# Seven products for both halves of the columns, with their sums of weights made in DRAM ahead of time

## The chip, the cores and the metric

The kernel runs on one core of a Trainium2 chip. A core has TensorE (PE in the profile, with its weight loads shown apart as PEld), VectorE (DVE), ScalarE (ACT), GpSimd (POOL) and SyncE (SP), and 16 DMA engines that all queues share. The metric is the device time of one execution in microseconds. The kernel before takes 2182.1 us (median of three runs, 2181.91 to 2182.17).

## The reference, cut to what matters

Two layers on 256 tokens of width 2048, all in float32. Layer 0 mixes with attention and pooling, layer 1 with an mLSTM, and each mixer is followed by a gated MLP:

```
x = x + mixed                                    # attention layer, then mLSTM layer
x = x + conv_ffn(rms_norm(x, norm_ffn[layer]), w_up[layer], conv_w[layer], conv_b[layer], w_down[layer])

u = x @ w_up                                     # 2048 -> 2 * 5632
u = c[0] * up[:, :-2] + c[1] * up[:, 1:-1] + c[2] * up[:, 2:] + conv_b
gate, val = jnp.split(u, 2, axis=-1)
return (jax.nn.silu(gate) * val) @ w_down        # 5632 -> 2048
```

The change concerns the last product, `(256 x 5632) @ (5632 x 2048)`.

## The kernel before, in words

**Products.** Every float32 operand is split into a high part and a rest, and a product is three matmuls: high by high, high by rest, rest by high. The activations are split once. The weights stream from DRAM in tiles of 128 x 1024 (512 KB): `Stream` loads a tile on SP's queue up to five tiles ahead, and splits it up to two tiles ahead (`split`, L110 to L126: a cast on ACT, L121, and a subtraction on DVE, L122). There are six buffers for raw and four for split tiles.

**The MLP.** The 44 blocks of 128 hidden columns are worked in six chunks (`FCH`, of 4, 8, 8, 8, 8, 8 blocks). For each block an up-projection takes four weight tiles (64 matmuls, `up`), then gather, convolution and gating run on ACT and DVE. While chunk c is projected up, the down product of chunk c - 1 is woven between its up-projections, in the order that `_ffn_plan` writes out. The output columns are four blocks of 512. Columns of the first half (blocks 0 and 1) come from plain blocks (`down`, tile `dn`): 8 K blocks x 2 row blocks x 3 matmuls = 48 a block.

**Seven products.** The second half of the columns (`_halves` gives `(1,)`) uses a form of block multiplication in which a 2 x 2 by 2 x 2 product takes seven block products instead of eight. A pair of K blocks, the two row blocks of 128 and the two column blocks of 512 make up the 2 x 2 blocks. `combine` forms sums of activations for a pair. `unit` of kind "A" does four products that need sums of weights, kind "B" three with plain weights. With weight blocks b11, b12, b21, b22 the A products need b11 + b12, b12 + b22, b11 + b12 + b22 and the sum of all four. These are formed as the tile arrives: a `Sum` tile is loaded by SP and the second summand is added by an accumulating DMA on POOL's queue (`prepare`, L104 to L108); the next tile, a `Chain`, is completed with two additions on DVE (L117, L118). A products collect in four PSUM banks, go to the accumulator `acc` or to the residual `x`, and `total` puts the accumulator together at the end. The last chunk uses plain blocks for all columns.

**Order.** PE runs in program order. A small clock, `Weave`, interleaves side tasks (generators, such as a head of attention) with the main stream: each matmul group advances it by its own time, and a task that yields d is resumed when d us of it have passed. So a task's delay sets where its instructions stand in the program. On ACT, DVE, POOL and SP the framework's planner (`schedule_with_timeline_sim=True`, L1325) then orders the instructions by a timeline of its own and by their data; only the very beginning is kept in program order on ACT, DVE and SP as well. Each engine executes its list in order, DMA issues included. A DMA issue waits on semaphores first: for its data and buffers, and for an earlier DMA that used the same completion semaphore.

**POOL's other work.** POOL computes the power -1/2 of every norm (`rsqrt`, L245): `ry_n0` for the first norm, `ry_qk` for the keys, `ry_qq0`, `ry_qq1`, `ry_qq2` for three blocks of four query heads. DVE multiplies with the result right after (L247 to L250).

Of the kernel before, what the change touches and what calls it, by code (L numbers as in the profile page):

```python
# [16 lines left out]
P = 128  # L17
# [14 lines left out]
FT = DFF // P  # L32
FCH = [4, 8, 8, 8, 8, 8]
CH = 8
BOTH = ()
NEG = -1.0e30
NGATE = 96 + 8
WARM = 5
# [31 lines left out]
        self.one, self.other = one, other  # L70


class Chain:


# [4 lines left out]
class Stream:  # L80
# [8 lines left out]
    def load(self, pieces=1):  # L89
        i = self.n_load  # L90
        self.n_load += 1
        src = self.srcs[i]
        if isinstance(src, Sum):
            i in self.w or self.prepare(i)
            return
        src = src.src if isinstance(src, Chain) else src
        width = src.shape[-1]
        n = width // pieces
        w = self.wpool.tile([P, CH * P], F32, tag="w", name=f"w{i}")
        for c in range(0, width, n):  # L100
            self.nc.sync.dma_start(w[:, c : c + n], src[:, c : c + n])
        self.w[i] = w, n, width

    def prepare(self, i):  # L104
        w = self.sums.tile([P, CH * P], F32, tag="sum", name=f"sum{i}")
        self.nc.sync.dma_start(w, self.srcs[i].one)
        self.nc.gpsimd.dma_start(w, self.srcs[i].other, accum_op=ALU.add)
        self.w[i] = w, CH * P, CH * P  # L108
# [80 lines left out]


@with_exitstack
def trunk(ctx: ExitStack, tc: tile.TileContext, gx, xT, xn, call, catt, cml, weights, out):
    nc = tc.nc
    v, a, g, pe = nc.vector, nc.scalar, nc.gpsimd, nc.tensor

# [506 lines left out]
    def mlstm_layer(norm, nxt):  # L702
        with ExitStack() as es:
# [171 lines left out]

            hns, done = {}, set()
            wv.add(norm.finish(), 6.0)
            for hp in range(MH // 2):
                vf = t1p.tile([P, 2, 512], F32, tag="vf", name=f"mvf{hp}")
                for c, n in ((0, MD + 32), (MD, MD)) if hp == 0 else ((0, 512),):  # L880
                    ps = mov_group(xx, f"mv{hp}_{c}", n)
                    if hp + c == 0:
                        wv.until(lambda: norm.rcol is not None)
                        wv.add(gates(ps))
                    n = min(n, 512 if hp else MD)
                    for t in range(2):
# [12 lines left out]
                wv.add(gated(mov_group(xx, f"mo{hp}"), [2 * hp, 2 * hp + 1]))  # L899
# [7 lines left out]
    def ffn_layer(layer, norm, nxt):  # L907
        with ExitStack() as es:
# [16 lines left out]
            def up(c, f, gt, i):  # L925
# [156 lines left out]

            wv.add(norm.finish(), 4.0)
            f, gts = 0, []
            for kind, c, i, *j in _ffn_plan():
                if kind == "up":
                    if i == 0:
                        gts.append(actp.tile([P, 8, 2, S], F32R, tag=f"B{c % 2}", name=f"g{layer}_{c}"))
                    up(c, f, gts[c], i)
                    f += 1  # L1090
                elif kind == "down":
                    down(c, i)
                elif kind == "two":
                    down_two(c)
                elif kind == "mix":
                    combine(c, i)
                else:
                    unit(kind, c, i, *j)
# [58 lines left out]
    return np.ascontiguousarray(t.transpose(4, 0, 2, 1, 3, 5)).reshape(FT * (KT // 4), P, CH * P)  # L1157


def _halves(c):  # L1160

    return () if c == len(FCH) - 1 else (0, 1) if c in BOTH else (1,)


def _ffn_plan():

    seq = []
    for c, n in enumerate(FCH):
        pairs = FCH[c - 1] // 2 if c else 0
        units = [(kind, c - 1, h, j) for h in (_halves(c - 1) if c else ()) for kind in "AB" for j in range(pairs)]
        per = max(1, len(units) // n)

        busy = {u[3]: k // per for k, u in enumerate(units) if u[0] == "A"}
        for i in range(n):
            seq.append(("up", c, i))
            seq += units[i * per : i * per + per]  # L1180
            if len(_halves(c - 1)) == 1:
                for b in range(2):
                    if pairs and i == (b + 1) * pairs // 2 - 1:
                        seq.append(("down", c - 1, b))
# [5 lines left out]
def _down_chunks(w):  # L1190


    out, k0 = [], 0
    for c, n in enumerate(FCH):
        rows = w[k0 * P : (k0 + n) * P]
        blocks = [_mov(rows[:, b * 512 : b * 512 + 512]) for b in range(NB) if b // 2 not in _halves(c)]
# [15 lines left out]
    return res  # L1212


def _ffn_weights(up, parts):

    down = iter(parts[0])
    out, u = [], 0
    for kind, c, i, *j in _ffn_plan():
        if kind == "up":  # L1220
            out += up[u : u + 4]
            u += 4
        elif kind in ("down", "two"):
            out += [next(down) for _ in range(FCH[c] // 2 * (2 if kind == "two" else 1))]
        elif kind != "mix":
            s0, s1, r, ba, bb = parts[1 + 5 * i : 6 + 5 * i]
            q = sum(FCH[:c]) // 2 + j[0]
            out += [Sum(s0[q], s1[q]), Chain(r[q])] if kind == "A" else [ba[q], bb[q]]
    return out


def _constants():
# [97 lines left out]
```

## Time and profile before

| | |
|---|---|
| median of three runs | 2182.1 us |
| the profiled execution | 2182.76 us, span 2181.0 us |
| PE busy | 2175.4 us (100%) |
| DVE busy | 1670.8 us (77%) |
| ACT busy | 1370.6 us (63%) |
| POOL busy | 59.3 us (3%) |
| DMA | 462.95 MB, mean 212 GB/s |
| granted TensorE clock | 1.0 |

The span is the profiled execution on the core itself; 1.8 us lie around it. By the timeline of PE attention ends at some 256 us, the first MLP at 975 us, the mLSTM layer at 1457 us, and the second MLP fills the rest. In lines of groups and of the timeline, `out<-in` names the tiles that are written and read, L121 is line 121 of the kernel, and what stands in brackets is the engine's idle time just before and what ended it. Rows of engine SPq, ACTq or POOLq are DMA issues on these queues.

### The profile page before, as it was taken

To read this page: it belongs to the slowest core of one execution; us is meant where nothing else is said; L and a number is where in the kernel's file an instruction comes from. 1 tells how busy PE (TensorE), PEld (TensorE's weight loads), DVE (VectorE), ACT (ScalarE), POOL (GpSimd) and SP (SyncE) were. 2 spreads that over 40 slices of the span, in tenths; PEclk is the share of its full clock that TensorE was granted. 3 is DMA by queue.
4 is the path that set the end of the run, shared out by engine and by line. 5 is a ranking of instruction groups with operands and counts; after the bars stand their busy time and mean duration, and the time that the engine had idled before them with its cause. 6 is when DMAs were issued, how large, how long until landed. Compare 5 with 4: busy or idle time off the path is not lost.

```text
span 2181.0 us, 31219 instructions
## 1 busy us (share of the span) xinstructions
PE 2175.4 (100%) x11508; PEld 1862.8 (85%) x11508; DVE 1670.8 (77%) x2366; ACT 1370.6 (63%) x2166; POOL 59.3 (3%) x76
## 2 busy tenths in 40 slices
PE   9999999999999999999999999999999999999999
PEld 7888888888888888889888888888888888888887
DVE  7686688887878788776777676668888787878776
ACT  7665576766767576666454554557676666757663
POOL 0010000000000000000000000000000000000000
PEclk9999999999999999999999999999999999999999
DMA  9556567676877766656465555756768677776664
GB/s 326 178 169 203 174 199 235 206 244 206 256 226 245 229 221 215 219 193 205 160 201 182 180 179 175 223 182 197 232 205 243 214 240 236 242 230 227 215 213 163
DMA packets 133595, 462.95 MB, mean 212 GB/s; under 512 B 14810, under 2 KB 17154, under 8 KB 133442
## 3 DMA queue, kind: packets, MB, share of 16 engines
q1 hardware_dynamic: 125024, 438.08, 60.0%
q0 software_dynamic: 5344, 19.14, 5.2%
q10 hardware_dynamic: 3074, 3.75, 0.7%
q8 instruction: 90, 1.47, 0.3%
q14 instruction: 63, 0.52, 0.1%
HBM read 458.76 MB, written 2.14 MB: 211 GB/s over the span
## 4 chain that ended last, share of the span: by engine, by line
PE 99%; DMA 1%; DVE 0%; ACT 0%; issue 0%; SPq 0%; DVEq 0%
PE up L238 44%; PE dn L238 12%; PE op L238 8%; PE pp L238 8%; PE mv L238 4%; PE mq L238 4%; PE mk L238 4%; PE mo L238 4%; PE qproj L238 3%; PE pool L238 1%; PE vproj L238 1%; PE kproj L238 1%; PE qk L238 1%; PE av L238 1%; PE end L238 0%; PE xt L289 0%
## 5 line engine op out<-in xcount | busy, mean ns | idle before, releaser
L122 DVE TENSOR_TENSOR hl<-w,hl 128x1024 fp32r<-128x1024 f32 (+2 forms) x808 | 952.4, 1192 | 258.4 <-ACT hl L121 255.9
L121 ACT CAST hl<-w 128x1024 fp32r<-128x1024 f32 (+2 forms) x807 | 816.1, 1028 | 464.4 <-PE up L238 146.0
L238 PE MATMUL up<-xx,hl 128*128 128x512 f32 (+1 forms) x5632 | 993.9, 337 | 0.4 <-DVE hl L122 0.4
L238 PEld LDWEIGHTS up<-xx,hl 128*128 128x128 f32 x5632 | 866.9, 188 | 131.1 <-DVE hl L122 0.8
L238 PE MATMUL dn<-hl,g 128*128 128x512 f32 x1200 | 277.3, 390 | 0.0
L238 PEld LDWEIGHTS dn<-hl,g 128*128 128x128 f32 x1200 | 224.8, 188 | 46.7
L401 ACT COPY tb_up<-up 128x512 f32<-128x512 f32 x88 | 51.7, 587 | 133.3 <-PE up L238 133.3
L238 PE MATMUL pp<-hl,s 128*128 128x512 f32 x432 | 111.2, 393 | 0.0
L936 ACT ACTIVATE y<-tb_up,cst 128x256 f32<-128x256 f32 x176 | 103.8, 590 | 0.0
L402 DVE TENSOR_TENSOR tb_up<-up,tb_up 128x512 f32<-128x512 f32 x88 | 60.7, 690 | 56.0 <-ACT tb_up L401 55.7
L937 DVE TENSOR_TENSOR y<-y,z 128x510 f32<-128x510 f32 x88 | 60.5, 688 | 49.7 <-ACT y L936 49.7
L934 ACT ACTIVATE z<-tb_up,cst 128x256 f32<-128x256 f32 x176 | 88.5, 503 | 11.2 <-DVE tb_up L929 10.8
L238 PE MATMUL mk<-xx,hl 128*128 128x512 f32 (+1 forms) x512 | 92.1, 337 | 0.0
L238 PE MATMUL mq<-xx,hl 128*128 128x512 f32 (+1 forms) x512 | 92.1, 337 | 0.0
L238 PE MATMUL mv<-hl,xx 128*128 128x512 f32 (+2 forms) x480 | 91.7, 350 | 0.0
L238 PE MATMUL op<-hl,cat 128*128 128x512 f32 x384 | 91.6, 393 | 0.0
L238 PEld LDWEIGHTS pp<-hl,s 128*128 128x128 f32 x432 | 78.5, 188 | 15.1
L238 PE MATMUL mo<-hl,xx 128*128 128x512 f32 x384 | 90.5, 391 | 0.0
L238 PE MATMUL op<-hl,mcat 128*128 128x512 f32 x384 | 89.5, 392 | 0.0
L238 PEld LDWEIGHTS mq<-xx,hl 128*128 128x128 f32 x512 | 79.2, 188 | 11.6
L238 PEld LDWEIGHTS mk<-xx,hl 128*128 128x128 f32 x512 | 79.0, 188 | 11.4
L238 PEld LDWEIGHTS mv<-hl,xx 128*128 128x128 f32 x480 | 78.3, 189 | 11.2
(234 smaller groups left out, 1987.3 us busy)
## 6 DMA issues: line engine op xcount, KB each, us to landing
w<-in_up SPq DMA_DIRECT2D x352, 512.0 KB, 4.3
w<-in_dn SPq DMA_DIRECT2D x176, 512.0 KB, 4.7
w<-in_m_in SPq DMA_DIRECT2D x124, 512.0 KB, 4.1
w<-in_a_in SPq DMA_DIRECT2D x46, 512.0 KB, 4.4
sum<-in_dn SPq DMA_DIRECT2D x36, 512.0 KB, 4.8
sum<-in_dn POOLq DMA_DIRECT2D x36, 512.0 KB, 7.7
w<-in_a_out SPq DMA_DIRECT2D x32, 512.0 KB, 3.5
w<-in_m_out SPq DMA_DIRECT2D x32, 512.0 KB, 4.2
```

The source lines that it names most:

```text
L121: (self.nc.vector.tensor_copy if i + c == 0 else self.nc.scalar.copy)(hl[:, 0, c : c + n], w[:, c : c + n])
L122: self.nc.vector.tensor_sub(hl[:, 1, c : c + n], w[:, c : c + n], hl[:, 0, c : c + n].bitcast(F32))
L238: pe.matmul(out_, lhsT, rhs, start=start, stop=stop, skip_group_check=True)
L401: a.copy(tb, ps[:, :, 1, :])
L402: v.tensor_add(tb, ps[:, :, 0, :], tb)
L934: a.activation(z[:, 0, j, :], u[:, j, :], AF.Copy, scale=cw(tl, 0))
L936: a.activation(y[:, j, :], u[:, j, :], AF.Identity, scale=cw(tl, 1), bias=cw(tl, 3))
L937: v.tensor_add(y[:, :, 1:S], y[:, :, 1:S], z[:, 0, :, 0 : S - 1])
```

## The change

`_halves` gives both halves of the columns for chunks 2, 3, 4 of layer 0 and chunks 1 to 4 of layer 1 (`BOTH`), seven chunks of the ten that use seven products at all. In these chunks the two plain blocks of the first half disappear, and A and B units for it take their place, four of each; `_ffn_plan` puts them in slots of their own: two A units in each of the first two slots, four B units in the third, four slots with one A unit of the second half, and four B units in the last.

For the first half the sums of weights are not formed as tiles arrive. `premix` forms them in DRAM scratch: for each of 28 pairs (12 in layer 0, 16 in layer 1) two DRAM to DRAM copies of 512 KB on ACT's queue, then on POOL's queue an accumulating DMA of 512 KB and two of 256 KB, each on the result of the one before. The tasks are handed to `Weave` at the head of the attention layer (one more every 26 us, and 26 us between a task's steps) and of the mLSTM layer (28 us). The units then load the finished tiles (`Made`) as plain weights. The sums' buffers go from two to three, those of the gated tiles from three to two.

```diff
-BOTH = ()
+BOTH = ((2, 3, 4), (1, 2, 3, 4))
...
-        src = src.src if isinstance(src, Chain) else src
+        src = src.src if isinstance(src, Chain) else src.ap if isinstance(src, Made) else src
...
-        w = self.sums.tile([P, CH * P], F32, tag="sum", name=f"sum{i}")
+        w = self.sums.tile([P, CH * P], F32, tag="sum", bufs=3, name=f"sum{i}")
...
+    scratch = pool("mixed", 1, space=bass.MemoryType.DRAM)
+
+    def premix(layer, gap):
+
+        def one(i, s0, s1, r, made):
+            m = scratch.tile([P, 2, CH * P], F32, tag=f"m{layer}{i}", name=f"m{layer}_{i}")
+            h = CH * P // 2
+            nc.scalar.dma_start(m[:, 0], s0)
+            nc.scalar.dma_start(m[:, 1], r)
+            yield gap
+            g.dma_start(m[:, 0], s1, accum_op=ALU.add)
+            yield gap
+            g.dma_start(m[:, 1, :h], m[:, 0, :h], accum_op=ALU.add)
+            yield gap
+            g.dma_start(m[:, 1, h:], m[:, 1, :h], accum_op=ALU.add)
+            for j in range(2):
+                made[j].ap = m[:, j]
+
+        for i, e in enumerate(mixes[layer]):
+            wv.add(one(i, *e), (i + 1) * gap)
...
             wv.add(k_block(ps))
             wv.tick(0.0)
+            premix(0, 26.0)
...
             wv.add(norm.finish(), 6.0)
+            premix(1, 28.0)
...
-                    quads[c, i // 2] = tp.tile([P, 4, P], F32, tag="silu", bufs=3, name=f"s{layer}_{f}")
+                    quads[c, i // 2] = tp.tile([P, 4, P], F32, tag="silu", name=f"s{layer}_{f}")
...
-        units = [(kind, c - 1, h, j) for h in (_halves(c - 1) if c else ()) for kind in "AB" for j in range(pairs)]
-        per = max(1, len(units) // n)
-
-        busy = {u[3]: k // per for k, u in enumerate(units) if u[0] == "A"}
+        halves = _halves(layer, c - 1)
+
+        def units(kind, h, js):
+            return [(kind, c - 1, h, j) for j in js]
+
+        if halves == (0, 1):
+            slots = [units("A", 0, (0, 1)), units("A", 0, (2, 3)), units("B", 0, range(4))]
+            slots += [units("A", 1, (j,)) for j in range(4)] + [units("B", 1, range(4))]
+        else:
+            slots = [units(kind, 1, (j,)) for kind in "AB" for j in range(pairs)]
+            for b in range(2 if pairs else 0):
+                slots[(b + 1) * pairs // 2 - 1].append(("down", c - 1, b))
+
+        busy = {u[3]: k for k, slot in enumerate(slots) for u in slot if u[0] == "A"}
...
+            if kind == "B":
+                out += [ba, bb]
+            elif i:
+                out += [Sum(s0, s1), Chain(r)]
+            else:
+                made = [Made(), Made()]
+                mixes.append((s0, s1, r, made))
+                out += made
```

More of the change, by code (lines that the diff above doesn't have):

```diff
@@ L191, in trunk @@
 @with_exitstack
-def trunk(ctx: ExitStack, tc: tile.TileContext, gx, xT, xn, call, catt, cml, weights, out):
+def trunk(ctx: ExitStack, tc: tile.TileContext, gx, xT, xn, call, catt, cml, weights, mixes, out):
     nc = tc.nc
@@ L1084, in ffn_layer @@
             f, gts = 0, []
-            for kind, c, i, *j in _ffn_plan():
+            for kind, c, i, *j in _ffn_plan(layer):
                 if kind == "up":
@@ L1157, in _up_chunks, with _halves, _ffn_plan @@
     return np.ascontiguousarray(t.transpose(4, 0, 2, 1, 3, 5)).reshape(FT * (KT // 4), P, CH * P)
[L1160 to L1165 removed]
+def _halves(layer, c):
+    return () if c in (-1, len(FCH) - 1) else (0, 1) if c in BOTH[layer] else (1,)
+def _ffn_plan(layer):
     seq = []
@@ L1173, in _ffn_plan @@
         pairs = FCH[c - 1] // 2 if c else 0
-        units = [(kind, c - 1, h, j) for h in (_halves(c - 1) if c else ()) for kind in "AB" for j in range(pairs)]
-        per = max(1, len(units) // n)
-        busy = {u[3]: k // per for k, u in enumerate(units) if u[0] == "A"}
+        halves = _halves(layer, c - 1)
[9 more added lines that the diff above has]
+        busy = {u[3]: k for k, slot in enumerate(slots) for u in slot if u[0] == "A"}
         for i in range(n):
             seq.append(("up", c, i))
[L1180 to L1184, printed above, removed]
+            seq += slots[i] if i < len(slots) else []
             if c < len(FCH) - 1:
@@ L1195, in _down_chunks @@
         rows = w[k0 * P : (k0 + n) * P]
-        blocks = [_mov(rows[:, b * 512 : b * 512 + 512]) for b in range(NB) if b // 2 not in _halves(c)]
+        blocks = [_mov(rows[:, b * 512 : b * 512 + 512]) for b in range(NB) if b // 2 not in _halves(layer, c)]
         if c == len(FCH) - 1:
@@ L1212, in _down_chunks, with _ffn_weights @@
     return res
-def _ffn_weights(up, parts):
+def _ffn_weights(layer, up, parts):
     down = iter(parts[0])
-    out, u = [], 0
-    for kind, c, i, *j in _ffn_plan():
+    out, u, mixes = [], 0, []
+    for kind, c, i, *j in _ffn_plan(layer):
         if kind == "up":
@@ L1225, in _ffn_weights @@
         elif kind != "mix":
[L1226 to L1229, printed above, removed]
+            s0, s1, r, ba, bb = (e[sum(FCH[:c]) // 2 + j[0]] for e in parts[1 + 5 * i : 6 + 5 * i])
+            if kind == "B":
[6 more added lines that the diff above has]
+                out += made
+    return out, mixes
 def _constants():
@@ L1307 @@
         arrays[f"up{l}"] = _up_chunks(i["w_up"][l])
-        for j, part in enumerate(_down_chunks(i["w_down"][l])):
+        for j, part in enumerate(_down_chunks(l, i["w_down"][l])):
             arrays[f"dn{l}{j}"] = part
@@ L1319, in ffn @@
     def ffn(l):
-        return _ffn_weights(chunks(f"up{l}"), [chunks(f"dn{l}{j}") for j in range(11)])
+        out, m = _ffn_weights(l, chunks(f"up{l}"), [chunks(f"dn{l}{j}") for j in range(11)])
+        mixes.append(m)
+        return out
+    mixes = []
     n = 3 * (MD + 32)
```

6 lines of the change are left out of this document (4 added, 2 removed).

## The prediction

> **What bounds the kernel now.** I read the page's engine table first, then what TensorE (PE) waited for, then the DMA queues, then the stages in windows.
>
> ```profile
> span 2181.0 us, 31219 instructions
> PE 2175.4 (100%) x11508; PEld 1862.8 (85%) x11508; DVE 1670.8 (77%) x2366; ACT 1370.6 (63%) x2166; POOL 59.3 (3%) x76
> ...
> q1 hardware_dynamic: 125024, 438.08, 60.0%
> q0 software_dynamic: 5344, 19.14, 5.2%
> ```
> ```profile
> PE up L238 <- DVE hl L122: 0.4, 1, 0.4
> ```
>
> PE is busy for the whole span, and the view of PE's waits has a single one for a split weight, of 0.4 us. So a matmul that is removed shortens the kernel by its own time, and nothing else can shorten it. It also means that whatever makes PE wait is added in full. The queue rows hold a price: plain loads (q1) take 60.0% for 438.08 MB, accumulating DMAs (nearly all of q0) 5.2% for 19.14 MB, so a byte that is accumulated costs (5.2/19.14)/(60.0/438.08) = 1.98 times a byte that is loaded.
>
> ```profile
> 0.00:32.00 32.00, 30.73 (x124) 24.53 (x125) 22.81 (x41) 22.65 (x47) 0.73 (x9) 1.00 0.97 378
> 32.00:115.00 83.00, 83.00 (x405) 69.42 (x404) 58.95 (x104) 54.03 (x117) 6.55 (x6) 1.00 0.63 196
> 0.00:115.00 115.00, 113.73 (x527) 93.95 (x528) 81.76 (x145) 76.68 (x162) 7.28 (x15) 1.00 0.73 247
> ...
> 1677.00:1808.00 131.00, 131.00 (x698) 112.29 (x697) 107.86 (x145) 88.43 (x138) 4.24 (x5) 1.00 0.73 234
> ```
>
> These are windows (columns: PE, PEld, DVE, ACT, POOL busy, clock, DMA share, GB/s). In the first 32 us the DMA engines are at 0.97 with 378 GB/s: that is their full speed on loads. Up to 115 us they move 115 x 247 = 28.4 MB. The last row is one K chunk of the second MLP: PE 131 of 131, VectorE (DVE) 108, ScalarE (ACT) 88.
>
> **The change, part by part.** *Matmuls removed.*
>
> ```profile
> 422.76 2.24 PE L238 MATMUL pp<-hl,s 128*128 128x512 f32 x9
> 424.84 0.85 PE L238 MATMUL pp<-hl,g 128*128 128x512 f32 x3
> 425.53 11.30 PE L238 MATMUL up<-xx,hl 128*128 128x512 f32 x64
> ...
> 439.44 11.04 PE L238 MATMUL dn<-hl,g 128*128 128x512 f32 x48
> 450.32 11.30 PE L238 MATMUL up<-xx,hl 128*128 128x512 f32 x64
> ...
> 500.15 1.53 PE L238 MATMUL pp<-hl,g 128*128 128x512 f32 x6
> 501.52 0.85 PE L238 MATMUL pp<-hl,s 128*128 128x512 f32 x3
> 502.21 11.30 PE L238 MATMUL up<-xx,hl 128*128 128x512 f32 x64
> ...
> 552.94 2.23 PE L238 MATMUL pp<-hl,s 128*128 128x512 f32 x9
> ```
>
> From start to start a plain block of 48 matmuls takes 450.32 - 439.44 = 10.88 us, an A unit 425.53 - 422.76 = 2.77, a B unit 502.21 - 500.15 = 2.06. In each of seven chunks two plain blocks (21.76 us) become four A and four B units (19.32): 2.44 us off, 17.1 us in all. This is the whole gain.
>
> *Splits and evictions added in the MLPs.*
>
> ```profile
> L122 DVE TENSOR_TENSOR hl<-w,hl 128x1024 fp32r<-128x1024 f32 x762 | 921.5, 1221 | 247.5 <-ACT hl L121 245.2
> L122 DVE TENSOR_TENSOR hl<-w,hl 128x512 fp32r<-128x512 f32 x40 | 27.4, 686 | 8.3 <-ACT hl L121 8.1
> L1006 DVE TENSOR_TENSOR x<-x,pp 128x512 f32<-128x512 f32 x10 | 6.8, 678 | 0.0
> L121 ACT CAST hl<-w 128x1024 fp32r<-128x1024 f32 (+2 forms) x807 | 816.1, 1028 | 464.4 <-PE up L238 146.0
> ```
>
> Seven products read 16 weight tiles a chunk where the plain blocks read 8: 28 more splits of 1024 and 28 of 512 columns, and 32 more PSUM sums. On DVE 28 x 1.221 + 28 x 0.686 + 32 x 0.678 = 75 us, 10.7 a chunk: 118.6 of some 128.6 us, 92%. On ACT at most 56 x 1.028 = 58 us, 8 a chunk: 96 of 128.6. Both stay under PE and I cost them at nothing; PE covers them, with 10 us a chunk to spare on DVE. The tight place is a slot with four B units at once, where DVE owes four 1024 and four 512 splits (7.6 us) in 8.2 us of PE besides the up-projection's own sums. If that cover fails in every such slot by a few us, the 17 us are gone; that is a rival. The third buffer for the sums and the second instead of third for the gated tiles cost nothing: in the plan a pair is combined at least one up-projection (11 us) before its buffer is asked for. The loads of the sums from DRAM are plain loads on SP's queue, six tiles' worth more a chunk (24 GB/s on 234).
>
> *The sums of weights made in DRAM.* 28 of them, each two copies of 512 KB on ACT's queue, then on POOL's queue one accumulate of 512 KB and two of 256 KB, each waiting for the one before. The source spreads them with gaps of 26 and 28. The built program does not: PE alone is kept in program order; the planner orders ACT and POOL by its own timeline, and these DMAs read nothing that is computed. This is POOL's built order (position, line, what):
>
> ```
> 10 L684 TensorCopy gcol<-gx0
> 11 L445 DMACopy m0_0<-in_dn02
> ...
> 49 L445 DMACopy m1_15<-in_dn12
> 50 L447 DMACopy m0_8<-m0_8
> 52 L251 TensorTensor ry_n0<-rv_n0,mhalf
> ...
> 68 L251 TensorTensor ry_qq0<-rv_qq0,mhalf
> ...
> 100 L449 DMACopy m1_15<-m1_15
> 101 L251 TensorTensor ry_qq1<-rv_qq1,mhalf
> ```
>
> 40 of the 84 accumulates, those of the last layer among them, stand ahead of the first norm's power, 53 ahead of `ry_qq0`, all 84 ahead of `ry_qq1`. On ACT all 56 copies stand ahead of the cast of the tenth weight tile, 52 of them ahead of the ninth, and each copy waits until an earlier DMA on its semaphore (eight for SP and ACT together; eight for POOL) has landed. The casts stand behind these waits. In the old profile the eighth and ninth tile's casts start at 19.95 us, the tenth's at 23.00:
>
> ```profile
> 19.95 1.99 ACT L121 CAST hl<-w 128x1024 fp32r<-128x1024 f32 x2
> 23.00 1.05 ACT L121 CAST hl<-w 128x1024 fp32r<-128x1024 f32 x1 [1.06 <-DMA w<-in_a_in]
> ```
> ```profile
> 41.10 0.72 POOL L245 TENSOR_TENSOR ry_n<-rv_n,mhalf 128x2 f32<-128x2 f32 x1 [36.24 <-DVE rv_n L243]
> ...
> 62.89 1.67 POOL L245 TENSOR_TENSOR ry_qq<-rv_qq,mhalf 128x8 f32<-128x8 f32 x1 [6.48 <-DVE rv_qq L243]
> 114.83 1.64 POOL L245 TENSOR_TENSOR ry_qq<-rv_qq,mhalf 128x8 f32<-128x8 f32 x1 [50.26 <-DVE rv_qq L243]
> ```
> ```profile
> 116.50 0.17 DVE L247 TENSOR_TENSOR re_qq<-ry_qq 128x8 f32<-128x8 f32 x1
> ...
> 117.99 1.22 DVE L122 TENSOR_TENSOR hl<-w,hl 128x1024 fp32r<-128x1024 f32 x1 [0.52 <-ACT hl L121]
> ```
>
> So now every one of these DMAs is on the path. The power of the second query block started at 114.83 us; 1.7 us later DVE reads it, and the next weight split stands behind it on DVE; PE has at most three split weights in hand. In the changed order that power cannot start before POOL has issued all 84 accumulates, and its semaphores let no more than eight be unfinished. Until then the DMA engines have to move:
> - what they moved by 115 us: 28.4 MB at 378 GB/s, 75 us;
> - 56 copies, 56 x 0.524 = 29.4 MB. No row shows DRAM to DRAM. From below the price of a load: 78 us. From above that of the accumulate, which also touches two places: 155. The copy has one end like a load and one more in DRAM, so it is near neither; I take the middle, 117;
> - 84 accumulates, 28 x 0.524 + 56 x 0.262 = 29.4 MB. The nearest row is the accumulate into SBUF, 1.98 x 78 = 154 us, which I take. From below the price of a load, 78; from above twice the row, if the DRAM end doubles it, 308.
>
> Sum 75 + 117 + 154 = 346 us against 114.8: 231 us late. All else in that stretch hides under it: the copies with the loads of the first 32 us take 32 + 117 = 149 us, or half as long again (224) if POOL's queue takes a third of the engines meanwhile; there ACT gets to the tenth cast, and the 92 us of work from it to `ry_qq1` (23.00 to 114.83) fit into what is left. POOL's issue is no limit:
>
> ```profile
> L107 POOL DMA_DIRECT2D sum<-in_dn x36: 852/855/926, 193.8 to 2028.8; - x36
> ```
>
> 84 x 0.86 = 72 us. Behind `ry_qq1` nothing is late any more: the scratch is complete long before it is first read, for the A unit that starts at 552.94 in the old profile.
>
> The Trainium skill, page "DMA: Bandwidth & Descriptors", section "Latency and other measured facts", gives 214 GB/s per direction as the full rate of copies between HBM tensors; by it the copies would take 29.4/214 = 137 us, an estimate, and the time would be 2417. No row of before shows such a copy; its figure lies between my two bounds.
>
> The sum stands against the profiled run's 2182.76 us (0.7 over the median, which I take off): 2182.8 + 231 - 17 - 0.7 = 2396 us.
>
> **The rivals.**
> 1. *The accumulates are cheap.* If into DRAM they cost as loads, 75 + 78 + 78 = 231 us, 116 late: 2281 us. For it: 1.98 is measured beside loads, whose waiting is in it. Against: loads wait in their price too.
> 2. *The accumulates are dear.* With the copies at 155 and the accumulates at 308, 538 us, 423 late: 2588 us. For it: source, old value and result all lie in DRAM. With the accumulates only half-way there (231) it is 2511.
> 3. *DVE takes the place of PE in the MLPs.* On top of the forecast, 14 slots of B units that stall by 1.2 us or more give back the 17 us: 2413 us and up, inside my range. Against: 10 us a chunk are left on DVE, and PE waited 0.4 us in all.
> 4. *Faster: the DMAs run spread out after all.* If what runs is not the built order but one DMA every 26 us or so, a sum (1.05 MB copied and 1.05 accumulated, worth 3.7 MB of load at my prices, 10 us) adds 0.38 to the share of 0.63 in the row from 32 to 115 us. That is full but just hidden, no power waits, and the time is 2182 - 17 = 2165 us. It decides only if the 84 accumulates are not ahead of `ry_qq1`. Against: in before, ACT's and POOL's records follow the built order instruction by instruction.
>
> **How the numbers follow.** The sum's own bounds, with the copies from 78 to 155 and the accumulates from 154 up to half-way to dear, span 2357 to 2511; I give this case 0.65. Cheap accumulates (2270 to 2357) 0.15, dear ones (over 2511) 0.16, spread out 0.03, and 0.01 for a result near no change. The likeliest is 2396. The range from 2285 to 2570 leaves out the spread case and the ends of the two others. Slower by over 0.2% (4.4 us, about what a measurement of this kernel can tell from no change): 0.96; faster 0.03; same 0.01.
>
> **What would show it.** Right: the DMA share at 0.95 or so for the first 300 to 400 us; the second `ry_qq` on POOL at about 346 us with accumulates up to it; PE mostly idle before that, released by ACT's and DVE's splits; the copies' casts stuck behind DMAs; 528 matmuls `dn` instead of 1200, and chunks of 128.6 us with DVE at 92%. Wrong: `ry_qq` near 115 us; a DMA share well under 0.9 while POOL waits (then latency, not throughput, sets the time, and it is longer); PE waiting for `hl` within the MLPs.

## The result, and the profile after

The changed kernel takes 2436.3 us (median of four runs, 2430.2 to 2442.4) against 2182.1 us: 1.1165 times as long, with a 95% interval of 1.1137 to 1.1193 (the brackets behind later ratios are such intervals too). The profiled execution took 2430.2 us with a span of 2428.4 us, which is 247.4 us over the span before.

First the page of the changed kernel, with the rows that answer to those of before:

```profile
span 2428.4 us, 31616 instructions
PE 2207.1 (91%) x11424; PEld 1864.8 (77%) x11424; DVE 1737.4 (72%) x2456; ACT 1416.6 (58%) x2228; POOL 128.3 (5%) x160
...
PEclk6556799999999999999999999999999999999999
DMA  9999985657676787876675555566676787878765
...
q1 hardware_dynamic: 133088, 460.10, 57.0%
q0 software_dynamic: 17440, 48.51, 11.5%
q10 hardware_dynamic: 11138, 33.11, 4.4%
```

PE now stands still for 9% of the span, and the DMA row is at its top for the first five slices of 61 us each. In the same slices the granted clock is 0.5 to 0.7. The queue rows price the new DMAs. Copies from DRAM to DRAM (most of q10) take 4.4% for 33.11 MB, loads 57.0% for 460.10 MB, so a copied byte costs 1.07 times a loaded one. The accumulating queue is at 11.5% for 48.51 MB, 1.91 times a load.

Next PE's waits, longest first (total us, times, longest):

```profile
PE kproj L244 <- ACT hl L127: 138.2, 8, 45.1
PE vproj L244 <- DVE hl L128: 20.0, 3, 18.5
PE qproj L244 <- ACT hl L127: 18.3, 2, 11.6
PE pp L244 <- DVE hl L128: 16.2, 15, 1.2
PE qproj L244 <- DVE hl L128: 7.7, 4, 3.7
PE pp L244 <- ACT hl L127: 6.4, 14, 0.5
```

The projections of attention wait for casts; that is the start of the kernel. The two rows of `pp` are new too, and they are the A and B units in the MLPs: 14 waits of 0.5 us and 15 of about 1.1.

POOL's timeline at the second and third query block:

```profile
324.27 0.81 POOL L449 DMA_DIRECT2D m<-m  x1 [1.74 <-DMA m<-m]
340.29 1.66 POOL L251 TENSOR_TENSOR ry_qq<-rv_qq,mhalf 128x8 f32<-128x8 f32 x1 [15.20 <-DVE rv_qq L249]
367.33 1.64 POOL L251 TENSOR_TENSOR ry_qq<-rv_qq,mhalf 128x8 f32<-128x8 f32 x1 [25.38 <-DVE rv_qq L249]
```

The last accumulate is issued at 324.27, and the second `ry_qq` starts at 340.29 instead of 114.83: 225.5 us late.

The starts of the norms' powers (`ry_n1`, `ry_n2`, `ry_n3`, and the end of the span) divide the kernel into stages. The table gives their lengths in us for this kernel and for the experiments whose stages matter below; each is the difference of two starts on POOL's timeline.

| kernel | to `ry_n1` | first MLP | mLSTM | second MLP |
|---|---|---|---|---|
| before | 259.1 | 723.2 | 478.0 | 720.7 |
| after | 487.9 | 729.5 | 478.0 | 733.0 |
| e1, MLP order alone | 259.0 | 730.2 | 478.0 | 732.7 |
| e3, copies kept in place | 269.8 | 730.2 | 478.0 | 732.2 |
| e5, B units in pairs | 262.2 | 724.0 | 479.5 | 722.8 |
| e8, the sums spread otherwise | 259.1 | 731.6 | 481.0 | 718.8 |
| e10, second layer only | 258.9 | 733.9 | 478.0 | 718.8 |
| e11, three chunks only | 258.9 | 722.5 | 478.0 | 722.4 |

The changed kernel loses 228.8 us up to `ry_n1`, 6.4 in the first MLP and 12.3 in the second, where 17 were to be won. Two questions follow: is the start's loss the place of the DMAs in their queues or their bytes, and what stops PE in the MLPs?

### The profile page after: what moved, and what is told of

Same layout as the page of the kernel before. It is cut to its first block, busy times and chain, and to the rows that moved or that the text cites. A ratio compares the mean times of both kernels' runs of the same rounds, so it can differ in the third digit from the quotient of the medians.

```text
span 2428.4 us, 31616 instructions
## 1 busy us (share of the span) xinstructions
PE 2207.1 (91%) x11424; PEld 1864.8 (77%) x11424; DVE 1737.4 (72%) x2456; ACT 1416.6 (58%) x2228; POOL 128.3 (5%) x160
## 3 DMA queue, kind: packets, MB, share of 16 engines
q1 hardware_dynamic: 133088, 460.10, 57.0%
q0 software_dynamic: 17440, 48.51, 11.5%
q10 hardware_dynamic: 11138, 33.11, 4.4%
## 4 chain that ended last, share of the span: by engine, by line
PE 82%; DMA 11%; DVE 3%; ACT 2%; issue 1%; POOL 0%; ACTq 0%; DVEq 0%; POOLq 0%
PE up L244 39%; PE pp L244 11%; DMA m<-in_dn 9%; PE op L244 7%; PE dn L244 5%; PE mv L244 4%; PE mq L244 4%; PE mk L244 4%; PE mo L244 4%; PE qproj L244 2%; DVE hl L128 2%; DMA m<-m 1%; DMA w<-in_dn 1%; PE vproj L244 1%; PE qk L244 0%
## 5 line engine op out<-in xcount | busy, mean ns | idle before, releaser
L128 DVE TENSOR_TENSOR hl<-w,hl 128x1024 fp32r<-128x1024 f32 (+2 forms) x864 | 1003.0, 1177 | 362.1 <-ACT hl L127 359.0
L127 ACT CAST hl<-w 128x1024 fp32r<-128x1024 f32 (+2 forms) x863 | 858.4, 1015 | 572.7 <-DMA m<-in_dn 131.1
L244 PE MATMUL pp<-hl,s 128*128 128x512 f32 x768 | 199.3, 395 | 0.2 <-DVE hl L128 0.2
L244 PE MATMUL pp<-hl,g 128*128 128x512 f32 x576 | 159.2, 399 | 22.4 <-DVE hl L128 16.0
L244 PE MATMUL kproj<-hl,xx 128*128 128x512 f32 x96 | 43.6, 615 | 141.2 <-ACT hl L127 138.2
L244 PEld LDWEIGHTS pp<-hl,s 128*128 128x128 f32 x768 | 141.2, 189 | 29.3 <-DVE hl L128 1.2
L244 PEld LDWEIGHTS pp<-hl,g 128*128 128x128 f32 x576 | 106.0, 189 | 53.3 <-DVE hl L128 20.5
L244 PE MATMUL dn<-hl,g 128*128 128x512 f32 x528 | 123.2, 392 | 0.0
L244 PEld LDWEIGHTS dn<-hl,g 128*128 128x128 f32 x528 | 99.2, 189 | 20.7
L244 PE MATMUL qproj<-hl,xx 128*128 128x512 f32 x288 | 77.6, 423 | 26.0 <-ACT hl L127 18.3
```

Of the source, the lines that this page charges most:

```text
L127: (self.nc.vector.tensor_copy if i + c == 0 else self.nc.scalar.copy)(hl[:, 0, c : c + n], w[:, c : c + n])
L128: self.nc.vector.tensor_sub(hl[:, 1, c : c + n], w[:, c : c + n], hl[:, 0, c : c + n].bitcast(F32))
L244: pe.matmul(out_, lhsT, rhs, start=start, stop=stop, skip_group_check=True)
```

## The experiments

Two theories stood at the outset. The first is the prediction's: the hoisted DMAs cost 230 us at the start and the MLPs give 17 back. The other is the prediction's third rival, which the `pp` waits suggest: the MLPs lose as well. The first two runs take the change apart.

**e1: the MLP order alone.** The 140 DMAs that make the sums are left out, and the first half's A units read tiles that were not summed.

```diff
-            premix(0, 26.0)
-            premix(1, 28.0)
...
+                made[0].ap, made[1].ap = s0, r
```

> Only the new order of products in the MLPs; the 140 DMAs that make the sums of weights in DRAM are left out, and the A units of the first half read plain tiles (so their products use weights that are not summed). From the traces (first MLP 6.4 us longer than before, second 12.3, where 17.1 us less were forecast) the new order alone should cost 19 us: 2201 us. By the prediction's step, with every split covered, it gains 17 us: 2165 us.

It took 2202.0 us, ratio 1.0094 (1.0079 to 1.0109). So the MLPs do lose 20 us, with nothing hoisted at all. PE's waits:

```profile
PE pp L244 <- DVE hl L128: 16.3, 15, 1.2
PE pp L244 <- ACT hl L127: 6.4, 14, 0.5
```

These are the changed kernel's `pp` rows again, to 0.1 us.

**e2: the sums alone.** The MLPs are those of before; the sums are made in DRAM and never read.

```diff
-BOTH = ((2, 3, 4), (1, 2, 3, 4))
+BOTH = ((), ())
+MIX = ((2, 3, 4), (1, 2, 3, 4))
...
+    for c in MIX[layer]:
+        for j in range(FCH[c] // 2):
+            s0, s1, r = (e[sum(FCH[:c]) // 2 + j] for e in parts[1:4])
+            mixes.append((s0, s1, r, [Made(), Made()]))
```

> Only the sums in DRAM, never read; the MLPs work as before. If the loss at the start is that of these DMAs alone (second block of queries 225 us late, first MLP norm 229 us late), 2182 + 229 = 2411 us, and with the 19 us of the MLPs it adds up to the changed kernel. If the two parts share a cost (buffers, loads of the scratch), it is under 2400 us.

It took 2413.9 us, ratio 1.106 (1.1043 to 1.1076): 232 us over before. With e1's 20 that makes 252 of the 254 measured. The parts add up, so they can be studied apart. Its second `ry_qq`:

```profile
341.67 1.66 POOL L252 TENSOR_TENSOR ry_qq<-rv_qq,mhalf 128x8 f32<-128x8 f32 x1 [15.43 <-DVE rv_qq L250]
```

**e3: the same DMAs, kept at their place in ACT's queue.** Accumulates stay free, but each needs its copies, so they follow.

```diff
-            nc.scalar.dma_start(m[:, 0], s0)
-            nc.scalar.dma_start(m[:, 1], r)
+            tc.keep_in_program_order(nc.scalar.dma_start(m[:, 0], s0))
+            tc.keep_in_program_order(nc.scalar.dma_start(m[:, 1], r))
```

> The changed kernel with its 56 copies kept on ACT's queue behind what stands ahead of them in the source, so that the sums are spread over the two layers; same bytes. If the place of the DMAs in the queues is what costs 229 us, attention is back within 10 us of before, and the time is that of the MLPs alone, 2201 to 2211 us. If the bytes themselves cost (28 sums of about 10 us of DMA time each beside the loads), the loss stays for a good part: 2300 us or more.

It took 2214.4 us, ratio 1.0149 (1.0134 to 1.0164), a little over the 2211 that was expected at most. The bytes, the number of DMAs and their accumulates are the same, and 222 of the 254 us are gone: the loss at the start comes from where the DMAs stand in the queues. What is left is the MLPs' 20 us and 10.6 us in attention, where chains of accumulates now stand ahead of the next norm's power (no idle time before it):

```profile
269.75 1.01 POOL L251 TENSOR_TENSOR ry_n<-rv_n,mhalf 128x2 f32<-128x2 f32 x1
```

**The MLPs' stall, in the trace.** One slot with four B units in the changed kernel's first MLP, on PE, DVE and ACT:

```profile
815.02 1.53 PE L244 MATMUL pp<-hl,g 128*128 128x512 f32 x6
...
821.78 0.51 PE L244 MATMUL pp<-hl,g 128*128 128x512 f32 x1 [0.46 <-ACT hl L127]
823.43 1.43 PE L244 MATMUL pp<-hl,g 128*128 128x512 f32 x5 [1.15 <-DVE hl L128]
824.70 0.86 PE L244 MATMUL pp<-hl,s 128*128 128x512 f32 x3
825.39 1.79 PE L244 MATMUL up<-xx,hl 128*128 128x512 f32 x9
```
```profile
817.72 1.83 DVE L128 TENSOR_TENSOR hl<-w,hl 128x1024 fp32r<-128x1024 f32 x2
820.83 0.69 DVE L966 TENSOR_TENSOR y<-y,z 128x510 f32<-128x510 f32 x1 [1.28 <-ACT y L965]
821.55 0.69 DVE L967 TENSOR_TENSOR y<-y,z 128x510 f32<-128x510 f32 x1
822.16 2.96 DVE L128 TENSOR_TENSOR hl<-w,hl 128x1024 fp32r<-128x1024 f32 x3
```
```profile
818.10 0.51 ACT L963 ACTIVATE z<-tb_up,cst 128x256 f32<-128x256 f32 x1
...
820.21 0.59 ACT L965 ACTIVATE y<-tb_up,cst 128x256 f32<-128x256 f32 x1
820.70 3.45 ACT L127 CAST hl<-w 128x1024 fp32r<-128x1024 f32 x4
```

Four units should take 4 x 2.06 = 8.24 us and take 825.39 - 815.02 = 10.37. ACT runs six activations of the convolution (818.10 to 820.7) before it casts the fourth unit's weights, and DVE, whose next instruction is an addition of the convolution, idles 1.28 us for them and only then splits. So the wait is not one for DVE's throughput. A B unit uses up two split tiles in 2.06 us, the up-projection four in 11.1, and the planned order of ACT and DVE has the convolution's work in that very place.

**e4: two units a slot.** It is built on e3. This needs a third buffer for gated tiles, and for room the sums go back to two.

```diff
-        w = self.sums.tile([P, CH * P], F32, tag="sum", bufs=3, name=f"sum{i}")
+        w = self.sums.tile([P, CH * P], F32, tag="sum", name=f"sum{i}")
...
-                    quads[c, i // 2] = tp.tile([P, 4, P], F32, tag="silu", name=f"s{layer}_{f}")
+                    quads[c, i // 2] = tp.tile([P, 4, P], F32, tag="silu", bufs=3, name=f"s{layer}_{f}")
...
-            slots = [units("A", 0, (0, 1)), units("A", 0, (2, 3)), units("B", 0, range(4))]
-            slots += [units("A", 1, (j,)) for j in range(4)] + [units("B", 1, range(4))]
...
+            seq += units[i * per : i * per + per]
```

> As e3_pinned, with two units after each up-projection in place of the four B units in one slot, three buffers for the gated tiles and two for the sums; the same instructions otherwise. If the stalls in the MLPs (some 2.1 us in each of 14 slots of four B units) come from the four units in a row, they go, and the 17 us of removed matmuls show: 2165 to 2175 us. If DVE's total load (88% in the MLPs) makes them, they stay: about 2200 us.

It took 2224.4 us, ratio 1.0195 (1.0178 to 1.0212), slower than e3. The waits of `pp` went down to 3.5 us, and others took their place, as PE's waits and DVE's show (total us, times, longest):

```profile
PE up L244 <- DVE hl L128: 26.5, 22, 4.4
```
```profile
DVE w L123 <- DMA sum<-in_dn: 35.5, 14, 5.8
```

A sum's loads come late 14 times, DVE waits for them in its queue, and the splits of the up-projection stand behind. The kernel before also has two buffers for the sums, and DVE's waits there show none for a sum. So it is two buffers together with this order that make the wait; e4 changes both at once and does not say which of them would do.

**e5: B units in pairs, three buffers for the sums.** All four A units of the first half go in one slot, so that the gated tiles need no third buffer. The copies are kept in place as in e3, and here all three accumulates of a sum too (one of the three edits is shown).

```diff
-            g.dma_start(m[:, 0], s1, accum_op=ALU.add)
+            tc.keep_in_program_order(g.dma_start(m[:, 0], s1, accum_op=ALU.add))
...
-            slots = [units("A", 0, (0, 1)), units("A", 0, (2, 3)), units("B", 0, range(4))]
-            slots += [units("A", 1, (j,)) for j in range(4)] + [units("B", 1, range(4))]
+            slots = [units("A", 0, range(4)), units("B", 0, (0, 1)), units("B", 0, (2, 3))]
+            slots += [units("A", 1, (0,)), units("A", 1, (1,)), units("A", 1, (2, 3))]
+            slots += [units("B", 1, (0, 1)), units("B", 1, (2, 3))]
```

> After, with the copies and the accumulates kept at their planned places on both queues, and with another layout of slots in the seven chunks: the four A units of the first half in one slot, no slot with more than two B units, the sums' three buffers kept. Theory: of the +20 us of the MLPs, the stalls of the B slots (some 2 us in each of 14) go and the 17 us of removed matmuls come through: before's 2182 less 17, plus at most the 10 us that the first stage lost with pinned copies: 2165 to 2178 us, PE's waits of pp for DVE's hl under 2 us in all. Rival: DVE at 92% of such a chunk is too full whatever the layout, and the wait moves to the up-projections as it did with two units a slot: 2195 to 2225 us, PE waiting 15 us or more for DVE's hl.

It took 2192.8 us, ratio 1.0049 (1.0035 to 1.0062). That is 22 us better than e3, but outside the theory's 2165 to 2178 and just under the rival's 2195 to 2225. By the table 15.6 of the 22 us lie in the two MLPs, and 7.6 in attention, where the accumulates now stand elsewhere. The B slots' waits are gone, but the new order has a cost of its own. A slot of four A units takes 12.1 to 12.7 us where four times 2.77 is 11.08, and one up-projection in each of these chunks takes 0.4 more than the usual 11.14. Two like A slots stand 129.16 us apart (1764.57 to 1893.73) against 130.16 before: 1.0 of the 2.44 us is won. Single late loads are much of the rest. The dearest is at the start of the second MLP, on the timelines of DVE and then of PE:

```profile
1529.97 0.69 DVE L123 TENSOR_TENSOR w<-w,sum 128x512 f32<-128x512 f32 x1 [6.41 <-DMA w<-in_dn]
```
```profile
1531.85 12.52 PE L244 MATMUL up<-xx,hl 128*128 128x256 f32 x62 [3.38 <-DVE hl L128]
```

There twelve accumulates ran right behind `ry_n3` on POOL, and the DMA share was 1.02 to 1.06 from 1510 to 1530.

**e6: the changed kernel with the copies, without the accumulates.**

```diff
-            g.dma_start(m[:, 0], s1, accum_op=ALU.add)
-            yield gap
-            g.dma_start(m[:, 1, :h], m[:, 0, :h], accum_op=ALU.add)
-            yield gap
-            g.dma_start(m[:, 1, h:], m[:, 1, :h], accum_op=ALU.add)
```

> After without the 84 accumulates: each scratch tile holds only the copied weights, so the first half's A units are fed with weights that were not summed; their number and size stay. Theory (what costs is the DMA work queued ahead of the first attention stage, on either queue): the casts from the tenth on wait until the 56 copies have landed, 32 us of loads and 29.4 MB at 3.2 us/MB (95 us), some 115 us against 23, so the second query block's power comes some 90 us late: 2182 + 20 + 90 = 2290 us, between 2270 and 2310. Rival A (POOL's queue alone sets it, the copies hide beside loads): 2200 to 2220. Rival B (the copies' waits set it all, the accumulates ran beside them): 2400 or more.

It took 2296.6 us, ratio 1.0526 (1.0511 to 1.054), where 2290 was expected. On its timelines, the cast of the tenth weight tile on ACT (the first of the three in this row) and POOL's second `ry_qq`:

```profile
114.82 2.93 ACT L127 CAST hl<-w 128x1024 fp32r<-128x1024 f32 x3
```
```profile
204.54 1.64 POOL L251 TENSOR_TENSOR ry_qq<-rv_qq,mhalf 128x8 f32<-128x8 f32 x1 [50.19 <-DVE rv_qq L249]
```

The cast starts at 114.8 us, as worked out, instead of 23.0, and the 89.7 us from there to `ry_qq` are the engines' work of before (91.8). So ACT's queue alone, blocked by copies that have to land, makes `ry_qq` 89.7 us late. The accumulates on POOL's queue account for the other 136.

**e7: the changed kernel with only the first layer's 12 sums at the start.**

```diff
-            nc.scalar.dma_start(m[:, 0], s0)
-            nc.scalar.dma_start(m[:, 1], r)
+            pin = (lambda e: tc.keep_in_program_order(e)) if layer else (lambda e: e)
+            pin(nc.scalar.dma_start(m[:, 0], s0))
+            pin(nc.scalar.dma_start(m[:, 1], r))
```

> After, with the copies of the second layer's 16 sums kept at their planned place in the mLSTM layer; the first layer's 12 sums still run at the start. Theory (the loss is the bytes ahead of the second query block's power): 75 us of loads, and 12/28 of 83 us of copies and of 150 us of accumulates, 175 us against 115, so 60 us late, with the 20 us of the MLPs 2262 us, between 2245 and 2285. Rival (the loss is not by bytes but by the waits of a few DMAs at the head, or by the low clock): near 2400 still, or under 2220.

It took 2304.2 us, ratio 1.0556 (1.0542 to 1.057), 42 us over the sum by bytes and outside its 2245 to 2285, but not where the rival has it either. Windows of the start (PE, PEld, DVE, ACT, POOL busy, clock, DMA share, GB/s), and POOL's rows:

```profile
150.00:180.00 30.00, 30.00 (x149) 25.10 (x148) 22.99 (x39) 17.48 (x27) 5.61 (x5) 1.00 1.03 313
180.00:210.00 30.00, 30.00 (x153) 25.24 (x153) 18.72 (x31) 19.21 (x46) 0.00 (x0) 1.00 0.48 155
```
```profile
133.13 0.72 POOL L251 TENSOR_TENSOR ry_n<-rv_n,mhalf 128x2 f32<-128x2 f32 x1 [23.66 <-DVE rv_n L249]
156.19 2.57 POOL L251 TENSOR_TENSOR ry_qq<-rv_qq,mhalf 128x8 f32<-128x8 f32 x1 [0.83 <-DVE rv_qq L249]
210.68 1.64 POOL L251 TENSOR_TENSOR ry_qq<-rv_qq,mhalf 128x8 f32<-128x8 f32 x1 [51.92 <-DVE rv_qq L249]
```

The bytes are indeed through at about 180 us, as 175 had been worked out. But the first `ry_qq` came only at 156, and from it to the second lie 54.5 us in which PE is the limit (52 before). Here the sum by bytes was a lower bound: the work of the engines that the same DMAs held up came on top as far as it didn't fit beside them.

**e8 and e9: can the rest be had?** e8 is e5 with other gaps:

```diff
-            premix(0, 26.0)
+            premix(0, 40.0)
...
-            premix(1, 28.0)
+            premix(1, 22.0)
```

> The layout of slots with B in pairs, copies and accumulates pinned, with the first layer's sums one every 40 us instead of 26 and the second layer's one every 22 instead of 28, so that fewer accumulates run in attention and only one behind the last norm's power, where twelve ran before. Theory (what is left of the loss is accumulates crowding the loads: attention +3 us, the starts of the two MLPs some +7, mLSTM +1.5): most of this 11 us goes, 2193 to about 2184, between 2178 and 2188, and PE's wait of 3.4 us at the start of the second MLP is gone. Rival (the DMA work costs the same wherever it is put): 2190 to 2196.

e9 is e8 with other slots:

```diff
-            slots = [units("A", 0, range(4)), units("B", 0, (0, 1)), units("B", 0, (2, 3))]
+            slots = [units("A", 0, (0, 1, 2)), units("A", 0, (3,)) + units("B", 0, (0,)), units("B", 0, (1, 2, 3))]
```

> As the spread one, but the first half's units in slots of three A, one A with one B, and three B, instead of four A, two B, two B. Theory: the slot of four A units costs 0.8 to 1.1 us in each of seven chunks since four units use up the split weights in hand; three units do not, so some 6 us less than the spread one: 2174 to 2182. Rival: three B units (two wide and two narrow tiles each) stall like four did: not less than the spread one.

e8 took 2192.3 us, ratio 1.005 (1.0036 to 1.0064): no gain on e5. Attention got its 3 us back and the second MLP 4, and the first MLP lost 7.6, the mLSTM layer 1.5; this is the rival. e9 took 2226.2 us, ratio 1.0203 (1.0189 to 1.0217). Three B units in a slot hardly wait themselves, but the up-projection behind them does, by PE's waits:

```profile
PE up L244 <- DVE hl L128: 30.5, 18, 4.0
```

**e10 and e11: fewer chunks.** Both have e5's slots and its DMAs kept in place. e10 has the second layer's four chunks alone, with its 16 sums made one every 70 us from the start on; e11 has three chunks, with 12 sums in the mLSTM layer.

```diff
-BOTH = ((2, 3, 4), (1, 2, 3, 4))
+BOTH = ((), (1, 2, 3, 4))
...
-            premix(0, 26.0)
+            premix(1, 70.0)
...
-            premix(1, 28.0)
+            pass
```

> Seven products for the first half in the second layer's four chunks alone (the first layer as before), B in pairs, copies and accumulates pinned, its 16 sums made one every 70 us from the start on, so that they spread over attention, the first MLP and the mLSTM layer. Theory (the removed matmuls pay where DVE has no more than two B units a slot and the sums do not crowd the loads): four chunks at 1.85 us less each, as steady chunks showed, less up to 4 us at the chunks' first slots: 2182 less 3 to 7, 2175 to 2179 us. Rival (every accumulate costs the loads about as much as it saves, wherever it lies): 2181 to 2188.

```diff
-BOTH = ((2, 3, 4), (1, 2, 3, 4))
+BOTH = ((), (2, 3, 4))
...
-            premix(0, 26.0)
+            pass
...
-            premix(1, 28.0)
+            premix(1, 30.0)
```

> Seven products for the first half in the second layer's last three chunks alone, B in pairs, copies and accumulates pinned, 12 sums in the mLSTM layer, one every 30 us; attention and the first MLP as before. Theory (the 10 us that the one-layer run lost in the first MLP were accumulates beside that MLP's loads): with nothing added there the first MLP takes 723 us again, the mLSTM layer loses at most 3 us, and three chunks of 129.2 us instead of 130.2 give 3 back: 2179 to 2184 us. Rival (the sums cost some 10 us wherever they lie): 2188 or more.

e10 took 2191.4 us, ratio 1.0045 (1.003 to 1.0059), slower than the theory and 3 us over the rival's 2188 as well. Its first MLP has the matmuls of before and took 10.8 us longer; beside the two pools' buffers, which e11 has too, only the spread DMAs are added there. e11 took 2182.4 us, ratio 0.9999 (0.999 to 1.0008): level with before. The time is within the expected 2179 to 2184, but not as worked out: the mLSTM layer lost nothing, and the three chunks won nothing (second MLP 722.4 us against 720.7).

These two runs also part the cost of the sums from that of the order of units. By POOL's timeline the last accumulate into DRAM is issued at 1405 us in e10 and at 1470 in e11, so their second MLPs run without such DMAs (but for the first 12 us in e11). Yet four chunks win 1.9 us there instead of 9.8, and three lose 1.7 instead of winning 7.3. That is the cost of the order itself, with the loads that it asks for. e11's waits of PE for splits, all of them in those chunks, are 4.2 of its 9.0 us:

```profile
PE pp L244 <- DVE hl L128: 2.7, 3, 1.1
PE up L244 <- DVE hl L128: 1.5, 4, 0.5
```

No version tried is faster than the kernel before.

## Why the prediction was right, and where not

The sign holds, and so does the mechanism at the start: 2396 was predicted, within 2285 to 2570, and it is 2436. What was forecast for the MLPs came out with the wrong sign. Against the profiled span the forecast misses 33.4 us. The start came out 5.5 us better than predicted (225.5 late, not 231), 3.3 us were lost between `ry_qq1` and `ry_n1`, and the MLPs are 35.6 worse (+18.6, not -17).

*Matmuls removed.* The count is right: 528 `dn` are left. The expected length of a chunk was not. The 131 us that I took as a chunk's length was the length of the window in the view, not that of a chunk. Two like B units in the second MLP of before stand 130.16 us apart:

```profile
1831.39 1.53 PE L238 MATMUL pp<-hl,g 128*128 128x512 f32 x6
...
1961.55 1.53 PE L238 MATMUL pp<-hl,g 128*128 128x512 f32 x6
```

With 2.44 off that is 127.7. In the changed kernel they stand 132.04 apart, and two B slots at 2.13 more (10.37 - 8.24) are 4.26 of the 4.3 us between: within that chunk nothing else is lost.

```profile
1970.80:2102.84 132.04, 128.83 (x683) 109.15 (x682) 116.20 (x157) 93.69 (x144) 3.46 (x4) 1.00 0.80 255
```

*Splits and evictions at nothing: this step failed.* DVE's load was about as worked out, 116 us in that chunk, 88%. The step took the mean load of a chunk and the sum of splits in a slot (7.6 in 8.2 us) as the test, and put the stall among the rivals (the third) with its price of at least 1.2 us in 14 slots. It is that rival that came: 0.46 + 1.15 us of waits in each of 14 slots and some 0.5 beside them, 2.13 in all. That is 29.8 of the 35.6 us; the other 6 are nine slots and up-projections that took 0.1 to 1.3 us more than their like, some after a short wait of their own and two with the matmuls behind a B slot's wait (11.7 and 11.5 us instead of 10.37). What the step left out is the order in which ACT and DVE do their work: the convolution's chain between the two engines stands ahead of the fourth unit's casts, and four split tiles are no more than two B units use up. The free 10 us of DVE lie elsewhere in the chunk. e5 took the four-B slots away and won 15.6 us over e3 in the MLPs; e4 and e9 show that other orders move the wait to the up-projection. None of them won the 17 us: in e5 a chunk keeps 1.0 of the 2.44.

*The third buffer for sums at nothing.* It didn't cost anything. e2 has the new buffers and the old order, and its MLPs take 722.5 and 720.7 us, against 723.2 and 720.7 before.

*The hoisted DMAs.* Their place in the queues is the cause: e3 has the same DMAs elsewhere and keeps 32 of 254 us. The terms were less right than their sum. Copies were taken at 117 us, in the middle between load and accumulate; by the queue rows they cost 1.07 times a load, 1.07 x 78 = 83 us, almost the lower bound. Accumulates cost 1.91 times a load in the changed kernel's mix, of which most go into DRAM, 149 us against 154 taken: a DRAM destination costs no more than one in SBUF. The sum becomes 75 + 83 + 149 = 307 us, by which the forecast would have been 2357. The last accumulate is issued at 324, with the DMA engines full until then (a share of 1.00 to 1.09 from 25 us on), so this sum is some 17 us short. `ry_qq1` comes at 340. The last 15.2 us are not DMA: POOL waits for DVE, that is for the engines' own chain. On ACT the last copy is issued just ahead of the cast of the tenth tile, which the prediction had at 149 to 224 us:

```profile
210.48 0.50 ACTq L443 DMA_DIRECT2D m<-in_dn  x1
213.69 2.92 ACT L127 CAST hl<-w 128x1024 fp32r<-128x1024 f32 x3
```

From there to `ry_qq1` there were 92 us of work, which "fit into what is left". They took 126.6 us and so ended last, by 15 us. On POOL the power `ry_qq0` stood behind accumulates, as the prediction's list has it, and came at 265.17, 51.5 us behind the cast (39.9 before); from it to `ry_qq1` it took 75.1 us (51.9 before), with the DMA engines full. In e6, without accumulates, the same stretch from the cast took 89.7. So the start's hit within 5.5 us is luck in part: copies and accumulates were taken 39 us too dear, and the 33 us that were missing made up for most of it. e7, where fewer bytes are hoisted, shows the engines' chain uncovered.

The Trainium skill, page "DMA: Bandwidth & Descriptors", section "Latency and other measured facts", states 214 GB/s per direction as the full rate of copies between HBM tensors, by which the 56 copies would take 137 us, an estimate. The runs don't agree: a copied byte costs 1.07 times a loaded one here, and by the time of their own packets the copies took some 95 us, 29.4 MB at 3.23 us each (4.4% of 2428 us over 33.11 MB). In e6 the last of the 56 is issued at 113.56 us, with the first loads beside them. By the page's price the forecast would have been 2417, nearer to the measured time, but for a wrong reason: what the forecast lacked were the MLPs.

*Nothing late behind `ry_qq1`.* Right to 3.3 us up to `ry_n1`, and exactly right in the mLSTM layer, 478.0 us in both. In the MLPs it isn't the scratch that comes late: e1, without these DMAs, has the same `pp` waits.

*The rivals.* Accumulates cheap (1.91, not 1) and dear (twice 1.98) are both refuted by the queue rows. The faster rival, DMAs spread out, is refuted as to what runs, and e5, e8 and e10 show its price was wrong too: these three take 2191 to 2193 us and not 2165. Two costs make the difference. The order of units takes 7.9 us in e10's second MLP and 9.0 in e11's, where next to none are made in DRAM any more. The sums take 10.8 us in e10's first MLP, where single loads come late beside accumulates, and nothing in e11's mLSTM layer at a gap of 30 us. The mean DMA share is 0.80 in both of these stages, so it isn't the share that tells them apart; what does is not shown. An order of units that keeps the 17 us was not found.

## What to carry to other kernels

A DMA that reads nothing computed has no natural place: unless it is tied down, whoever orders the queue may put all of them ahead of the first real work, so read the built order on each queue, then price the bytes that stand ahead of the first waiting instruction, and add the engine work that the same DMAs hold up. A gain in matmuls on a PE-bound kernel is only had if split weights arrive in the order in which PE burns them: test the slot with the densest weights against the buffers in hand and the engine's own order, not against its mean load. And a mean DMA share under 1 does not make added DMA work free: in e10's first MLP, where the share rose from 0.70 to 0.80, a few loads that came late cost PE 10.8 us.

## What the runs showed of the hardware that was not expected

The granted clock falls while PE starves, and what little PE does then takes longer. Two windows of the changed kernel, with the columns as above:

```profile
25.00:100.00 75.00, 17.32 (x36) 11.31 (x36) 7.21 (x11) 6.76 (x11) 11.26 (x14) 0.57 1.02 272
100.00:125.00 25.00, 0.00 (x0) 0.00 (x0) 0.00 (x0) 0.00 (x0) 4.33 (x6) 0.50 1.04 255
```

The same 96 matmuls `kproj`, as a group in the profile before and in the one of the changed kernel (busy us, mean ns):

```profile
L238 PE MATMUL kproj<-hl,xx 128*128 128x512 f32 x96 | 22.9, 395 | 0.0
```
```profile
L244 PE MATMUL kproj<-hl,xx 128*128 128x512 f32 x96 | 43.6, 615 | 141.2 <-ACT hl L127 138.2
```

PE's busy time is 2207.1 us against 2175.4, though 17 us of matmuls were taken out, so 49 us were added, 20.7 of them in `kproj`. They lie where PE waits for casts anyway; whether the low clock made the start longer was not tried.

A short idle time can be enough. In e10 PE idles 1.84 us before 62 matmuls of an up-projection, in e8 1.35 us before 62 of another. The timelines of e10 and e8, and then two windows of e10:

```profile
472.52 12.51 PE L244 MATMUL up<-xx,hl 128*128 128x256 f32 x62 [1.84 <-DVE hl L128]
```
```profile
303.93 10.95 PE L244 MATMUL up<-xx,hl 128*128 128x256 f32 x62 [1.35 <-DVE hl L128]
```
```profile
472.50:476.00 3.50, 3.48 (x15) 3.06 (x16) 3.47 (x4) 2.17 (x6) 0.32 (x1) 0.68 0.69 111
476.00:479.50 3.50, 3.50 (x18) 3.03 (x18) 2.98 (x5) 2.73 (x6) 0.00 (x0) 0.83 1.03 318
```

Behind the longer wait the clock is 0.68 and 0.83 on the mean of two stretches of 3.5 us (0.50 from 474 to 476), and the 62 matmuls take 1.56 us more. So a wait of 1.84 us cost 3.4. The idle time alone doesn't decide it: in the changed kernel the same 0.46 + 1.15 us stand in all 14 slots with four B units, and the clock fell clearly behind two of them (0.62 from 2112 to 2116), whose slots took 11.7 and 11.5 us instead of 10.37. The Trainium skill, page "TensorE: Matmul & The Clock Gate", section "What's actually happening", has the clock fall to half after an idle window of about 3.4 us that runs freely. The fall to 0.50 in an idle stretch agrees. That it can follow 1.84 us of idle time, about half of that window, does not, and here the measurement decides.
